# The last row tile of a matmul with layer norm: sums finished in PSUM by TensorE, two quarters scaled by ScalarE

## The chip, the cores and the metric

The kernel runs on one core of a Trainium2 chip. The metric is the device time of one execution in microseconds; of several executions the median is given. Before the change it is 246.81 us, the median of 3 runs from 246.68 to 247.35. A profile is one further execution, recorded by the hardware profiler.

## The reference

```python
m, k, n = 2048, 2048, 2048
x = np.matmul(a, b)                                # float32
mean = np.mean(x, axis=-1, keepdims=True)
var = np.var(x, axis=-1, keepdims=True)
normalized = (x - mean) / np.sqrt(var + eps)
return (gamma * normalized + beta).astype(np.float32)
```

`gamma` and `beta` have one value for each column, mean and variance one for each row; `eps` is 1e-5.

## The kernel before

The output is made in 16 row tiles of 128 rows, each in four quarters of 512 columns. A quarter is one PSUM bank, filled by 16 fp16 products (L85). The first five row tiles are worked on together while `b` arrives and is cast to fp16; from then on all of `b` lies in SBUF as `b16`, and the row tiles 5 to 15 follow one by one. Their rows of `a` are loaded with a cast by GpSimd's queue (L340) and turned by a transposing DMA on SP's queue (L407).

For each quarter `evacuate` (L95, L96) has ScalarE copy the bank to SBUF, to the tile `x`, and VectorE take its statistics. After the fourth quarter `stats` (L102 to L106) aggregates them to mean and variance (`mv`), adds eps (`ve`) and has ScalarE take the root (`sq`). The normalisation of a row tile is queued in two pieces (`queue_norm`) and run by VectorE while TensorE fills the next tile's banks. The schedule is manual: every engine runs its instructions in the order in which the program writes them, SP's stores too. The PSUM pool has eight buffers, taken in turn.

The last row tile (i = 15) has no next tile to hide behind, and `finish_row` writes its end out by hand. Quarters 0 to 2 were evacuated as usual, and `scaled` (L357) has already multiplied them by gamma in place. Quarter 3 stays in PSUM. After its last product:

- VectorE takes its statistics from PSUM (L364), then aggregates (L102) and adds eps (L104); ScalarE takes the root (L106). TensorE runs eight products of zeros meanwhile (`filler`, L236).
- VectorE centres quarter 3 and multiplies it by gamma (L367), inverts the root (`inv`, L127: `rstd`) and makes `nm` = -mean * rstd (L372).
- TensorE turns `nm` from a column to a row by a product with `ident32` (L375), and ScalarE copies the row into row 0 of `lead` (L376); row 1 of `lead` was set to ones at the start.
- For q = 1 and 2 TensorE multiplies `lead` with the rows (gamma, beta) in `rows_gb` (L380), in fp32: `w[q]` = nm * gamma + beta, as a full bank. For q = 0 VectorE makes the same as `shift` (L385) from `gamma_b` and `beta_b`, which hold gamma and beta on all partitions.
- VectorE finishes quarter 3 (`scale`, L117) and quarters 0, 1 and 2 (L390: x * rstd + w), and SP stores each quarter when it is done (`store`, L123), in the order 3, 0, 1, 2.

After the last store has landed, the program closes with waits and semaphore work.

Of the kernel before, what the change touches and what calls it, by code (L numbers as in the profile page):

```python
# [9 lines left out]
FP32 = mybir.dt.float32  # L10
FP16 = mybir.dt.float16
AluOp = mybir.AluOpType
ActFn = mybir.ActivationFunctionType
# [3 lines left out]
def kernel(  # L17
# [9 lines left out]
    nc = tc.nc  # L27
    P = 128
# [5 lines left out]
    NB = 512  # L34
# [20 lines left out]
    stat = ctx.enter_context(tc.tile_pool(name="stat", bufs=8))  # L55
    psum = ctx.enter_context(tc.tile_pool(name="psum", bufs=8, space=bass.MemoryType.PSUM))
# [4 lines left out]
    zeros = konst.tile([P, NB], FP16)  # L61
    eps_t = konst.tile([P, 1], FP32)
# [6 lines left out]
    xs = [None] * n_mt  # L69
    bnst = [None] * n_mt  # L70
    acc = {}

    def bank(name):
        return psum.tile([P, NB], FP32, tag="ps", name=name)
# [25 lines left out]
    def stats(i):  # L100
        mv = stat.tile([P, 2], FP32, tag="mv", name=f"mv{i}")
        nc.vector.bn_aggr(mv, bnst[i])  # L102
        ve = stat.tile([P, 1], FP32, tag="ve", name=f"ve{i}")
        nc.vector.tensor_tensor(ve, mv[:, 1:2], eps_t, AluOp.add)  # L104
        sq = stat.tile([P, 1], FP32, tag="sq", name=f"sq{i}")
        nc.scalar.activation(sq, ve, ActFn.Sqrt)  # L106
        return mv, sq
# [7 lines left out]
    def scale(i, q, rstd):  # L115
        qs = ds(q * NB, NB)
        nc.vector.scalar_tensor_tensor(  # L117
            xs[i][:, qs], xs[i][:, qs], rstd, beta_b[:, qs],
            AluOp.mult, AluOp.add)

    def store(i, q0, nq):
        s = ds(q0 * NB, nq * NB)
        nc.sync.dma_start(out[ts(i, P), s], xs[i][:, s])  # L123

    def inv(i, sq):
        rstd = stat.tile([P, 1], FP32, tag="rstd", name=f"rstd{i}")
        nc.vector.reciprocal(rstd, sq)  # L127
        return rstd
# [105 lines left out]
    def filler(n, to=None):  # L234
        for _ in range(n):
            nc.tensor.matmul(warm if to is None else to, zeros[:, 0:P], zeros, start=True, stop=True)  # L236
# [106 lines left out]
    rows_gb = [stg.tile([2, 2, NB], FP32, tag="st", name=f"gb{h}") for h in (0, 1)]  # L343
    ident32 = stg.tile([P, P], FP32, tag="st", name="ident32")
    nc.vector.tensor_copy(ident32, ident)
    shift = stg.tile([P, NB], FP32, tag="st", name="shift")
    lead = konst.tile([2, P], FP32)
    nc.vector.memset(lead, 1.0)
    for h in (0, 1):
        for m, vec in enumerate((gamma, beta)):  # L350
            nc.sync.dma_start(
                rows_gb[h][m:m + 1, :, :],
                vec[ds(h * NH, NH)].rearrange("(o t n) -> o t n", o=1, t=2))

    def scaled(i, q):
        qs = ds(q * NB, NB)
        nc.vector.tensor_tensor(xs[i][:, qs], xs[i][:, qs], gamma_b[:, qs], AluOp.mult)  # L357

    def finish_row(i):


        q3 = ds(3 * NB, NB)
        last_acc = acc[i, 3]
        nc.vector.bn_stats(bnst[i][:, 3, :], last_acc)  # L364
        filler(8, bank("warm2"))
        mv, sq = stats(i)
        nc.vector.scalar_tensor_tensor(  # L367
            xs[i][:, q3], last_acc, mv[:, 0:1], gamma_b[:, q3],
            AluOp.subtract, AluOp.mult)
        rstd = inv(i, sq)  # L370
        nm = stat.tile([P, 1], FP32, tag="nm", name="nm")
        nc.vector.scalar_tensor_tensor(  # L372
            nm, mv[:, 0:1], -1.0, rstd, AluOp.mult, AluOp.mult)
        nm_ps = psum.tile([1, P], FP32, tag="ps", name="nm_ps")
        nc.tensor.matmul(nm_ps, nm, ident32, start=True, stop=True)  # L375
        nc.scalar.copy(lead[0:1, :], nm_ps)  # L376
        w = {}
        for q in (1, 2):
            w[q] = bank(f"w{q}")
            nc.tensor.matmul(  # L380
                w[q], lead, rows_gb[q // 2][:, q % 2, :], start=True, stop=True)
        scale(i, 3, rstd)
        store(i, 3, 1)
        q0 = ds(0, NB)
        nc.vector.scalar_tensor_tensor(  # L385
            shift, gamma_b[:, q0], nm, beta_b[:, q0], AluOp.mult, AluOp.add)
        w[0] = shift
        for q in range(3):
            qs = ds(q * NB, NB)
            nc.vector.scalar_tensor_tensor(  # L390
                xs[i][:, qs], xs[i][:, qs], rstd, w[q], AluOp.mult, AluOp.add)
            store(i, q, 1)

    def quarter(i, q):
        for kt in range(n_kt):
# [20 lines left out]
    for i in range(R, n_mt):  # L416
        last = i == n_mt - 1
        turn_ahead(i + 2)
        for q in range(n_nb):
            quarter(i, q)  # L420
            if last and q == n_nb - 1:
                break
            evacuate(i, q)
            if q < n_nb - 1:
                drain(1)
            if last:
                scaled(i, q)
        if last:
            drain(len(backlog))
            finish_row(i)  # L430
        else:
            close(i)
# [35 lines left out]
```

## Time and profile before

| | us |
|---|---|
| median of 3 runs (lowest, highest) | 246.81 (246.68, 247.35) |
| the profiled execution | 246.63 |
| its span, from the first to the last instruction | 244.6 |
| TensorE busy | 236.8 (97%) |
| VectorE busy | 175.2 (72%) |
| ScalarE busy | 52.6 (21%) |
| GpSimd busy | 7.2 (3%) |
| start of the last tile's last statistics (L364) | 235.06 |
| issue of the last store | 240.83 |

All times in the profile are counted from the start of the span. The 246.63 us hold the span and some 2 us around it. Engines are named PE (TensorE; PEld its weight loads), DVE (VectorE), ACT (ScalarE), POOL (GpSimd) and SP, whose queue issues the stores. A row of the timeline gives start, duration, engine, line and operation, what it writes and reads, and in brackets the idle time before it with what ended it. The chain of waits goes back from the last instruction: at each step to what released it, or to the instruction before it on its engine. The granted clock of TensorE is a share of its full speed, 0.992 over the whole span.

### The profile page before, as it was taken

The page shows a single profiled execution, that of the slowest core. Times are in us where ns is not written, and L with a number is a line of the kernel's source. Part 1 is how long each engine was busy: PE and PEld are TensorE (multiplying, and loading weights), DVE is VectorE, ACT ScalarE, POOL GpSimd, SP SyncE. Part 2 cuts the span into 40 slices and gives each one's busy share as a digit, 9 for nine tenths or more (in the row PEclk, how much of TensorE's full clock was granted, in tenths as well). Part 3 has the DMA queues.
Part 4 walks back from the last instruction along what each step waited for, and adds up shares of the span by engine and source line. Part 5 has one row for each costly group of instructions (what it writes and reads, how often), then busy time and mean ns, then how long its engine had stood idle before and what let it go on. Part 6 is the DMA issues. An engine that isn't in the chain of part 4 may idle for free.

```text
span 244.6 us, 2975 instructions
## 1 busy us (share of the span) xinstructions
PE 236.8 (97%) x1137; PEld 108.0 (44%) x1137; DVE 175.2 (72%) x310; ACT 52.6 (21%) x96; POOL 7.2 (3%) x17
## 2 busy tenths in 40 slices
PE   7899999999999999999999999999999999999982
PEld 2344555444444444444444444444444444444430
DVE  1554554949997679999999995937557391947873
ACT  2457446400000011112111211112111211112100
POOL 0000000000300100000000000000000000000000
PEclk9999999999999999999999999999999999999996
DMA  4999999999999999899979897683907144120405
GB/s 125 398 386 385 388 387 385 316 357 375 331 271 179 158 131 201 196 316 205 263 189 283 147 298 222 149 200 71 256 4 190 68 123 137 74 97 0 175 1 172
DMA packets 41190, 52.64 MB, mean 215 GB/s; under 512 B 24404, under 2 KB 24404, under 8 KB 40920
## 3 DMA queue, kind: packets, MB, share of 16 engines
q1 hardware_dynamic: 39592, 46.68, 60.5%
q0 software_dynamic: 1584, 5.77, 15.4%
q8 instruction: 9, 0.15, 0.2%
q14 instruction: 5, 0.04, 0.0%
HBM read 35.67 MB, written 16.78 MB: 214 GB/s over the span
## 4 chain that ended last, share of the span: by engine, by line
PE 94%; DMA 2%; DVE 1%; ACT 0%; SPq 0%; issue 0%
PE acc L85 90%; DMA st<-in_a_dram 2%; PE tps L243 2%; PE w L380 1%; PE warm L236 1%; DVE x L390 0%; DVE bnst L364 0%; DVE x L367 0%; ACT at L245 0%; DVE a16s L186 0%; SPq L198 0%; PE nm_ps L375 0%; SPq L184 0%; DVE mv L102 0%; ACT lead L376 0%
## 5 line engine op out<-in xcount | busy, mean ns | idle before, releaser
L85 PE MATMUL acc<-b,at 128*128 128x512 f16 x1024 | 223.5, 379 | 0.7 <-DVE b L199 0.4
L85 PEld LDWEIGHTS <-at 128*128 128x128 f16 x1024 | 99.7, 98 | 119.7 <-ACT at L245 2.1
L96 DVE BATCH_NORM_STATS2 bnst<-x 128x6 f32<-128x512 f32 x48 | 33.0, 690 | 34.1 <-ACT x L95 33.9
L95 ACT COPY x<-acc 128x512 f32<-128x512 f32 x48 | 28.1, 586 | 107.8 <-PE acc L85 107.8
L117 DVE SCALAR_TENSOR_TENSOR x<-x,rstd,beta_b 128x512 f32<-128x512 f32 x61 | 43.1, 748 | 0.5
L111 DVE SCALAR_TENSOR_TENSOR x<-x,mv,gamma_b 128x512 f32<-128x512 f32 x60 | 42.1, 743 | 0.0
L205 DVE CAST b<-stb 128x1024 f16<-128x1024 f32 x30 | 20.4, 687 | 13.0 <-DMA stb<-in_b_dram 12.9
L106 ACT ACTIVATE sq<-ve 128x1 f32<-128x1 f32 x16 | 3.2, 203 | 55.5 <-DVE ve L104 55.5
L245 ACT COPY at<-tps 128x512 f16<-128x512 f16 (+1 forms) x14 | 10.8, 768 | 14.1 <-PE tps L243 14.0
L265 DVE TENSOR_TENSOR x<-acc,x 128x512 f32<-128x512 f32 x15 | 10.3, 686 | 3.0 <-PE acc L85 2.7
L266 DVE BATCH_NORM_STATS2 bnst<-x 128x6 f32<-128x512 f32 x15 | 10.4, 694 | 0.5
L236 PE MATMUL warm<-zeros 128*128 128x512 f16 x27 | 9.0, 463 | 1.2 <-DVE zeros L152 1.2
L340 POOL DMA_DIRECT2D a<-in_a_dram x11 | 6.4, 587 | 91.6 <-DMA at<-a 91.3
L261 ACT COPY x<-acc 128x512 f32<-128x512 f32 x15 | 7.6, 606 | 6.0 <-PE acc L85 6.0
L243 PEld LDWEIGHTS <-a16s 128*128 128x128 f16 x80 | 5.4, 98 | 4.7 <-DVE a16s L186 2.4
L243 PE MATMUL tps<-ident,a16s 128*128 128x128 f16 x80 | 6.8, 219 | 0.4 <-DVE a16s L186 0.3
L194 DVE CAST a16s<-sta 128x1024 f16<-128x1024 f32 x6 | 4.2, 694 | 4.0 <-DMA sta<-in_a_dram 4.0
L186 DVE CAST a16s<-st 128x512 f16<-128x512 f32 x8 | 3.4, 427 | 5.0 <-DMA st<-in_a_dram 4.8
L236 PEld LDWEIGHTS <-zeros 128*128 128x128 f16 x27 | 2.9, 113 | 4.6 <-issue 2.2
L102 DVE BATCH_NORM_AGGREGATE mv<-bnst 128x2 f32<-128x24 f32 x16 | 4.2, 264 | 0.5
L199 DVE CAST b<-st 128x512 f16<-128x512 f32 x4 | 1.7, 427 | 1.8 <-DMA st<-in_b_dram 1.8
L104 DVE TENSOR_TENSOR ve<-mv,eps_t 128x1 f32<-128x1 f32 x16 | 2.6, 160 | 0.5
(26 smaller groups left out, 16.9 us busy)
## 6 DMA issues: line engine op xcount, KB each, us to landing
stb<-in_b_dram SPq DMA_DIRECT2D x30, 512.0 KB, 6.5
out_dram<-x SPq DMA_DIRECT2D x30, 512.0 KB, 3.1
a<-in_a_dram POOLq DMA_DIRECT2D x11, 512.0 KB, 6.9
sta<-in_a_dram SPq DMA_DIRECT2D x6, 512.0 KB, 6.6
st<-in_a_dram SPq DMA_DIRECT2D x8, 256.0 KB, 6.3
st<-in_b_dram SPq DMA_DIRECT2D x4, 256.0 KB, 6.1
gamma_b<-in_gamma_dram SPq DMA_DIRECT2D x1, 1024.0 KB, 8.0
beta_b<-in_beta_dram SPq DMA_DIRECT2D x1, 1024.0 KB, 10.3
```

The source lines that it names most:

```text
L85: nc.tensor.matmul(acc[i, q], at(i)[:, kt, :], b16[:, kt, ds(q * NB, NB)], start=first, stop=last,)
L95: nc.scalar.copy(xs[i][:, qs], acc[i, q])
L96: nc.vector.bn_stats(bnst[i][:, q, :], xs[i][:, qs])
L111: nc.vector.scalar_tensor_tensor(xs[i][:, qs], xs[i][:, qs], mv[:, 0:1], gamma_b[:, qs], AluOp.subtract, AluOp.mult)
L117: nc.vector.scalar_tensor_tensor(xs[i][:, qs], xs[i][:, qs], rstd, beta_b[:, qs], AluOp.mult, AluOp.add)
L205: nc.vector.tensor_copy(b16[:, k:k + 2, ds(q * NB, NB)], st)
L236: nc.tensor.matmul(warm if to is None else to, zeros[:, 0:P], zeros, start=True, stop=True)
L243: nc.tensor.transpose(t_ps[:, m, j, :], a16_of[i, c][:, ts(j, P)], ident)
L245: nc.scalar.copy(pair[i0 // 2][:, ds(i0 % 2, n), ds(c * KC, KC), :], t_ps)
L261: nc.scalar.copy(xs[p][:, ds(q * NB, NB)], acc.pop((p, q)))
L265: nc.vector.tensor_tensor(xs[p][:, qs], acc[p, q], xs[p][:, qs], AluOp.add)
L266: nc.vector.bn_stats(bnst[p][:, q, :], xs[p][:, qs])
```

## The change

It concerns `finish_row` and what prepares it. With s = sqrt(var + eps), the result is (x * gamma - mean * gamma + s * beta) / s. For quarters 1 and 2 the bracket is now formed in PSUM: a product of zeros opens the bank `y_ps[q]` (L373), ScalarE copies the already multiplied quarter over it (L374, L382), and TensorE adds the product of `lead` with `rows_gb` (L384). `lead` now holds the rows mean and s, which come from one transposition of the tile `mv` (L380, L381), and the gamma rows of `rows_gb` get their sign changed by GpSimd at the start (L353). The root is written in place of the variance, with eps as its bias (L378). ScalarE then multiplies the banks by `rstd` on the way to SBUF (L398, L404). Quarters 3 and 0 stay with VectorE, and `nm` is made after quarter 3 is done. The stores go out in the order 3, 1, 0, 2. There are two products of zeros to open the banks and four fillers in place of eight fillers. Lines here are those of the changed file.

```diff
     lead = konst.tile([2, P], FP32)
-    nc.vector.memset(lead, 1.0)
     for h in (0, 1):
         for m, vec in enumerate((gamma, beta)):
             nc.sync.dma_start(
                 rows_gb[h][m:m + 1, :, :],
                 vec[ds(h * NH, NH)].rearrange("(o t n) -> o t n", o=1, t=2))
+        nc.gpsimd.tensor_scalar(
+            rows_gb[h][0:1, :, :], rows_gb[h][0:1, :, :], -1.0, None, AluOp.mult)
+
+    y_ps = {}
...
         nc.vector.bn_stats(bnst[i][:, 3, :], last_acc)
-        filler(8, bank("warm2"))
-        mv, sq = stats(i)
+        for q in (1, 2):
+            y_ps[q] = bank(f"y{q}")
+            nc.tensor.matmul(y_ps[q], zeros[:, 0:P], zeros, start=True, stop=False)
+        nc.scalar.copy(y_ps[1], xs[i][:, ds(NB, NB)])
+        filler(4, bank("warm2"))
+        mv = stat.tile([P, 2], FP32, tag="mv", name="mv_last")
+        nc.vector.bn_aggr(mv, bnst[i])
+        nc.scalar.activation(mv[:, 1:2], mv[:, 1:2], ActFn.Sqrt, bias=eps_t)
+        ms_ps = psum.tile([2, P], FP32, tag="ps", name="ms_ps")
+        nc.tensor.matmul(ms_ps, mv, ident32, start=True, stop=True)
+        nc.scalar.copy(lead, ms_ps)
+        nc.scalar.copy(y_ps[2], xs[i][:, ds(2 * NB, NB)])
+        for q in (1, 2):
+            nc.tensor.matmul(
+                y_ps[q], lead, rows_gb[q // 2][:, q % 2, :], start=False, stop=True)
         nc.vector.scalar_tensor_tensor(
             xs[i][:, q3], last_acc, mv[:, 0:1], gamma_b[:, q3],
             AluOp.subtract, AluOp.mult)
-        rstd = inv(i, sq)
-        nm = stat.tile([P, 1], FP32, tag="nm", name="nm")
-        nc.vector.scalar_tensor_tensor(
-            nm, mv[:, 0:1], -1.0, rstd, AluOp.mult, AluOp.mult)
-        nm_ps = psum.tile([1, P], FP32, tag="ps", name="nm_ps")
-        nc.tensor.matmul(nm_ps, nm, ident32, start=True, stop=True)
-        nc.scalar.copy(lead[0:1, :], nm_ps)
-        w = {}
-        for q in (1, 2):
-            w[q] = bank(f"w{q}")
-            nc.tensor.matmul(
-                w[q], lead, rows_gb[q // 2][:, q % 2, :], start=True, stop=True)
+        rstd = inv(i, mv[:, 1:2])
         scale(i, 3, rstd)
         store(i, 3, 1)
+        nm = stat.tile([P, 1], FP32, tag="nm", name="nm")
+        nc.vector.scalar_tensor_tensor(
+            nm, mv[:, 0:1], -1.0, rstd, AluOp.mult, AluOp.mult)
         q0 = ds(0, NB)
         nc.vector.scalar_tensor_tensor(
             shift, gamma_b[:, q0], nm, beta_b[:, q0], AluOp.mult, AluOp.add)
-        w[0] = shift
-        for q in range(3):
-            qs = ds(q * NB, NB)
-            nc.vector.scalar_tensor_tensor(
-                xs[i][:, qs], xs[i][:, qs], rstd, w[q], AluOp.mult, AluOp.add)
-            store(i, q, 1)
+        nc.scalar.activation(
+            xs[i][:, ds(NB, NB)], y_ps[1], ActFn.Copy, scale=rstd)
+        store(i, 1, 1)
+        nc.vector.scalar_tensor_tensor(
+            xs[i][:, q0], xs[i][:, q0], rstd, shift, AluOp.mult, AluOp.add)
+        store(i, 0, 1)
+        nc.scalar.activation(
+            xs[i][:, ds(2 * NB, NB)], y_ps[2], ActFn.Copy, scale=rstd)
+        store(i, 2, 1)
```

More of the change, by code (lines that the diff above doesn't have):

```diff
@@ L369, in finish_row @@
             AluOp.subtract, AluOp.mult)
-        rstd = inv(i, sq)
+        rstd = inv(i, mv[:, 1:2])
+        scale(i, 3, rstd)
+        store(i, 3, 1)
         nm = stat.tile([P, 1], FP32, tag="nm", name="nm")
@@ L373, in finish_row @@
             nm, mv[:, 0:1], -1.0, rstd, AluOp.mult, AluOp.mult)
-        nm_ps = psum.tile([1, P], FP32, tag="ps", name="nm_ps")
-        nc.tensor.matmul(nm_ps, nm, ident32, start=True, stop=True)
-        nc.scalar.copy(lead[0:1, :], nm_ps)
-        w = {}
-        for q in (1, 2):
-            w[q] = bank(f"w{q}")
-            nc.tensor.matmul(
-                w[q], lead, rows_gb[q // 2][:, q % 2, :], start=True, stop=True)
-        scale(i, 3, rstd)
-        store(i, 3, 1)
         q0 = ds(0, NB)
```

## The prediction

> **What bounds the kernel now.** I read the busy line and the forty slices first. TensorE is busy for 97% of the span and every slice but the first and the last few is full, so up to about 235 us only TensorE's work counts. The chain that ended last says the same: 90% of the span is products of L85. The change touches nothing of that; it rewrites what follows the last product. So the question is one of some nine microseconds at the end, and the view to read is the chain of waits in order of time, from its last piece of L85 on (start, duration, what):
>
> ```profile
> 214.94 20.09 PE acc L85 x93
> ...
> 235.06 0.71 DVE bnst L364
> ...
> 235.79 0.27 DVE mv L102
> ...
> 236.08 0.16 DVE ve L104
> 236.24 0.66 DVE x L367
> ...
> 237.31 0.39 PE nm_ps L375 x2
> ...
> 237.73 0.26 ACT lead L376
> ...
> 238.04 1.99 PE w L380 x4
> ...
> 240.06 0.75 DVE x L390
> ```
>
> The reader is to see one serial path: statistics of the last quarter, the row's mean and 1/sqrt, a transposition on TensorE (nm_ps), a copy (lead), 1.99 us of fp32 products (w), one VectorE pass, one store. The timeline fills in what runs beside it:
>
> ```profile
> 236.34 0.20 ACT L106 ACTIVATE sq<-ve 128x1 f32<-128x1 f32 x1 [4.15 <-DVE ve L104]
> 236.82 0.15 DVE L127 RECIPROCAL rstd<-sq 128x1 f32<-128x1 f32 x1
> 237.01 0.16 DVE L372 SCALAR_TENSOR_TENSOR nm<-mv,rstd 128x1 f32<-128x1 f32 x1
> 237.09 0.75 DVE L117 SCALAR_TENSOR_TENSOR x<-x,rstd,beta_b 128x512 f32<-128x512 f32 x1
> ...
> 237.75 0.75 DVE L385 SCALAR_TENSOR_TENSOR shift<-gamma_b,nm,beta_b 128x512 f32<-128x512 f32 x1
> ```
>
> and SP's own rows give the last store:
>
> ```profile
> 240.83 0.33 SPq L123 DMA_DIRECT2D out_dram<-x  x1
> ```
>
> The four last stores are issued at 237.86, 239.31, 239.97 and 240.83. The first three land 2.45, 2.63 and 2.69 us later; the last, at their 2.62, at 243.45. The span ends at 244.6, so about 1.15 us of closing work follows the last landing whatever the kernel does before it. The transfers' own row, in forty slices of the stretch 237.5 to 244.6, is the other thing to see:
>
> ```profile
> GB/s 0 0 0 0 0 0 92 358 404 369 254 0 0 0 69 346 381 381 358 381 323 300 323 231 346 312 335 219 127 0 0 0 0 0 0 0 0 0 0 0
> ```
>
> The quarter stored first moves alone at up to 404 GB/s; the other three follow each other from 240.0 to 242.65 with no gap. That stream is already nearly closed, which limits what an earlier issue can win.
>
> **The change, step by step.**
>
> *Statistics to transposition.* The add of eps (L104) goes; ScalarE takes it as the bias of the root. The mean and root are then transposed as they stand, so neither 1/sqrt nor nm is on the way to TensorE. Aggregation ends at 236.05. The root began 0.10 after its producer (236.24 to 236.34) and took 0.20: now 236.15 to 236.35. The transposition began 0.14 after nm and took 0.38; the first weights have two columns instead of one, which I cost at nothing: 236.49 to 236.87. ScalarE's copy to lead took 0.26 after 0.04, two partitions instead of one: 236.91 to 237.17. Before it ended at 237.99, so the products start 0.82 earlier.
>
> *Ahead of that.* TensorE now runs two zeroing products and four fillers instead of eight fillers, 0.216 us apart (the eight start 234.85 to 236.37), so it is free by 236.35, before 236.49. A copy of quarter 1 into PSUM stands in ScalarE's queue ahead of the root. It can start when the first zeroing product is done, near 235.30. No row has ScalarE writing a whole quarter to PSUM. Nearest are ScalarE's copies out of PSUM of the same size, 0.586 us; bounds are 0.20 (the root's fixed part) and 1.01 (the 128x1024 copy). I take 0.59: it ends at 235.9, 0.25 before the root needs the engine. At 1.01 the root is late by some 0.2. The copy of quarter 2 follows lead: 237.17 to 237.76; only the second product waits for it, at about 238.3. Both are covered.
>
> *Products.* The same two fp32 products with two rows: four passes, 1.98 in all, the first two done after 1.12. That they add to PSUM instead of starting there I cost at nothing, as L85 adds in fifteen of sixteen products. Started at 237.22, y1 is done at 238.34, y2 at 239.20 (w was done at 240.02).
>
> *The scaling.* ScalarE now does quarters 1 and 2, VectorE 3 and 0. A scaled ScalarE pass of this shape has no row. The copy at 0.586 and the one-element root at 0.203 bound it: 0.59 below, and the root plus a whole copy, 0.79, above. I take 0.63, nearer to the copy. Quarter 1: 238.38 to 239.01. Quarter 2: 239.24 to 239.87, against 240.06 to 240.81.
> [...]
> [...]
>
> *VectorE.* Without L104 and nm ahead, the centring of quarter 3 starts at 236.08, 1/sqrt at 236.75, its scaling runs 236.93 to 237.68 (before 237.84), store at 237.70. Then nm, shift and quarter 0: 237.60, 237.79 and 238.58 to 239.33. Quarter 0 is 0.05 later than before, but no longer ahead of two more passes.
>
> *SP's queue.* The order is now quarters 3, 1, 0, 2, each issue 0.33 us; the closest two issues in the trace, at 63.13 and 63.48, lie 0.35 apart, and I allow 0.42. Quarter 1 goes at 239.03; quarter 0 waits behind it and goes at 239.45; quarter 2 at 239.89. The last issue is **0.94 us earlier** than 240.83.
>
> *Early parts.* VectorE loses one memset. GpSimd gets two sign changes of 1x1024 behind its last load issue, which is over by 163.4. No row shows their length; even 10 us each would be done 50 us before TensorE reads them. Should they slow VectorE there, its idle time takes it up: from the slice of 163 us on its digits in the page's forty slices are 3, 7, 5, 5.
>
> *Landing.* Quarters 1, 0 and 2 are now issued within 0.86 us, not 1.52. 262,144 bytes at some 385 GB/s (the lone store's full slices are 358 to 404) take 0.68 us, so they queue. The first would land at 239.03 + 2.55 = 241.58, the last not before 241.58 + 2 x 0.68 = 242.94. With the 0.73 and 0.79 that lay between landings in the trace it is 243.10. Against 243.45 that is 0.51 or 0.35 us. If the transfers overlap as if each were alone, it is 239.89 + 2.62 = 242.51, a gain of the whole 0.94. I take **0.55**, near the queued price.
>
> **The sum.** Profiled execution: 246.63 us, span 244.6. 246.63 - 0.55 = 246.08. The median shown is 246.81, 0.18 above that execution, so on the median's scale the forecast is **246.25 us**, 0.23% faster. About 0.3%, or 0.74 us, is what a measurement of this kernel can tell from no change.
>
> **The rivals.**
>
> 1. *The transfers don't queue.* For: the stores are 2.45 to 2.69 us each, of which only 0.7 is data. Against: the slices from 240.0 to 242.65 show no gap at a spacing of 0.66 and 0.86. Gain 0.94: 245.87.
> 2. *ScalarE eats the gain.* It is now serial from the root to quarter 2: five passes. At 0.79 for each scaling, and 1.01 for each copy into PSUM, the root is 0.2 late and the last scaling 0.16 longer; of the 0.94 remain 0.58 at the issue, and a stream that is then less dense lands 0.2 to 0.4 earlier, or none if landings stretch. 246.4 to 246.8.
> 3. *TensorE's clock falls before the products are done: slower.* The granted clock is 1.00 in 237 to 240 and 0.57 on average in 240 to 244.6, which is one full speed to 240.6 and half after it, only 0.6 after the last fp32 pass; those passes did not hold it. Two fillers fewer may let it fall earlier. Each pass then takes 0.43 more; the gain at the issue is gone from the third slow pass on (a fall before about 237.8), and with all four slow y2 ends 1.7 later, the store leaves 0.8 after 240.83: 247.6. Against: in the trace the fall came 3.9 us after the last filler; the same delay from 236.3 is 240.2, a whole 1.0 after y2 is done. [...]
> 4. *It does not do what it says*: an early part shifts, or the path ends elsewhere (quarter 0's store, say) and nothing is won: 246.8.
>
> **Chances.** Forecast with queued stores, 245.95 to 246.55: 0.52. Rival 1: 0.24. Rival 2: 0.14. Rival 3: 0.05. Rival 4: 0.05. Faster by over 0.3% (below 246.07) is nearly all of rival 1 and a part of the forecast: 0.30. Slower by over 0.3% is rival 3 and some of 4: 0.08. Within: 0.62. For 8 in 10 the range leaves out rival 3 and the ends: from 245.65 (245.87 less the 0.18 between median and execution, rounded down) to 246.95 (nothing won, and a run a little above the median).
>
> **What would show it.** [...] Then the slices of the transfers: a closed stream of three stores near 385 GB/s, the last landing near 242.9. It is wrong if the passes are 0.86 apart (rival 3), if the scaled passes are near 0.8 or the root starts after 236.3 (rival 2), or if the last landing keeps 2.6 us from its issue (rival 1).

## The result, and the profile after

The changed kernel takes 246.66 us (median of 21 runs, 246.35 to 246.97), the kernel before 246.93 us on the same chips (21 runs, 246.65 to 247.8). The ratio is 0.9985 with a 95% interval from 0.9979 to 0.9991: a gain of 0.37 us, between 0.22 and 0.52 (the two medians alone differ by 0.27). That is inside the 0.3% within which the prediction called the two equal; the interval shows that it is a gain all the same.

The span of the profiled execution, 244.7 us, is no shorter than before. The reason lies at the other end: its last tile's statistics start at 235.37 instead of 235.06, because the first loads came 0.3 us later (the first block of `b` landed at 6.76 instead of 6.45). In the twelve profiles of this case that start lies between 235.06 and 235.84, in kernels with almost the same code up to there. What follows it repeats far better: in two profiles of the changed kernel the last landing comes 8.141 and 8.142 us after it. So everything below is counted **from the start of the last statistics (T)**. From T to the end of the span it was 9.57 us; now it is 9.31.

The chain of waits of the changed kernel, in order of time (start, duration, what), from the last products of L85 on:

```profile
214.83 20.52 PE acc L85 x95
...
235.37 0.71 DVE bnst L370
...
236.10 0.27 DVE mv_last L377
...
236.40 0.30 ACT mv_last L378
...
236.75 0.39 PE ms_ps L380 x2
...
237.16 0.26 ACT lead L381
237.43 0.14 issue
237.56 1.96 PE y L384 x4
...
239.55 0.69 ACT x L404
```

Between the root (mv_last L378) and the transposition nothing of VectorE is left, and the last piece is ScalarE's scaled pass. The products start 2.19 us after T instead of 2.98 and end 4.14 after it instead of 4.96. SP's rows give the last issue:

```profile
240.31 0.40 SPq L123 DMA_DIRECT2D out_dram<-x  x1
```

That is T + 4.94, against T + 5.78 before: 0.84 us won at the issue. Now the transfers, in forty slices of 0.175 us from 237.6 to 244.6:

```profile
GB/s 0 0 0 0 0 0 0 257 386 386 386 82 0 0 0 328 374 398 398 328 410 328 351 363 258 257 293 222 176 12 0 0 0 0 0 0 0 0 0 0
```

Fifteen slices in a row are filled, from 240.2 to 242.8, at up to 410 GB/s first and under 300 at the end. The landing of a store is its event in the trace; for the last store it shows only as the end of SP's last wait for a store: 243.51, T + 8.14, against T + 8.40. Of 0.84 us at the issue, 0.26 arrive at the landing. The last store now takes 3.2 us from issue to landing, not 2.6.

### The profile page after: what moved, and what is told of

It is laid out like the page before. It is cut to its first block, busy times and chain, and to the rows that moved or that the text cites. A ratio compares the mean times of both kernels' runs of the same rounds, so it can differ in the third digit from the quotient of the medians.

```text
span 244.7 us, 2976 instructions
## 1 busy us (share of the span) xinstructions
PE 236.4 (97%) x1135; PEld 107.8 (44%) x1135; DVE 173.7 (71%) x306; ACT 55.1 (23%) x100; POOL 12.6 (5%) x19
## 4 chain that ended last, share of the span: by engine, by line
PE 94%; DMA 2%; ACT 1%; DVE 1%; SPq 0%; issue 0%
PE acc L85 90%; DMA st<-in_a_dram 2%; PE tps L243 2%; PE y L384 1%; PE warm L236 1%; DVE bnst L370 0%; ACT x L404 0%; ACT at L245 0%; DVE a16s L186 0%; SPq L198 0%; PE ms_ps L380 0%; SPq L184 0%; ACT mv_last L378 0%; DVE mv_last L377 0%; ACT lead L381 0%
## 5 line engine op out<-in xcount | busy, mean ns | idle before, releaser
L85 PE MATMUL acc<-b,at 128*128 128x512 f16 x1024 | 223.5, 379 | 1.1 <-DVE b L199 0.8
L85 PEld LDWEIGHTS <-at 128*128 128x128 f16 x1024 | 99.7, 98 | 119.7 <-ACT at L245 2.1
L236 PE MATMUL warm<-zeros 128*128 128x512 f16 x23 | 8.2, 478 | 1.2 <-DVE zeros L152 1.2
L353 POOL TENSOR_SCALAR gb<-gb 1x1024 f32<-1x1024 f32 x2 | 5.5, 2764 | 0.0
```

Of the source, the lines that this page charges most:

```text
L85: nc.tensor.matmul(acc[i, q], at(i)[:, kt, :], b16[:, kt, ds(q * NB, NB)], start=first, stop=last,)
```

## The experiments

**Theory S**: the last three stores form a closed stream, that is, their transfers follow each other without an empty slice. Its start and what each store adds set the last landing; when the last of them is issued hardly matters. **Rival L**: a landing comes a set time after its own issue, and this time grew from 2.6 to 3.2 for another reason. The table has what the profiles show, in us after T: the issues of the last tile's stores in their order with the quarter, the last landing, and the timed result; each ratio is to runs of the kernel before that were taken with the row's own runs.

| kernel | issues (quarter) | last landing | median, ratio to before (95%) |
|---|---|---|---|
| before | 2.80 (3), 4.25 (0), 4.92 (1), 5.78 (2) | 8.40 | 246.93 |
| changed | 2.66 (3), 4.03 (1), 4.46 (0), 4.94 (2) | 8.14 | 246.66, 0.9985 (0.9979 to 0.9991) |
| e1 | 2.66 (3), 4.04 (1), 4.89 (2) | 7.38 | 245.59, 0.9948 (0.9935 to 0.9961) |
| e2 | 2.67 (3), 4.31 (0), 4.97 (1), 5.63 (2) | 8.45 | 246.89, 0.9994 (0.9985 to 1.0002) |
| e3 | 2.67 (3), 4.04 (1), 4.46 (0), 4.94 (2) | 8.16 | 246.76, 0.9990 (0.9980 to 1.0001) |
| e4 | 2.67 (3), 3.24 (1), 4.31 (0), 4.74 (2) | 7.52 | 245.94, 0.9953 (0.9942 to 0.9965) |
| e5 | 2.67 (3), 4.04 (1), 4.46 (0), 5.47 (2) | 8.16 | 246.64, 0.9987 (0.9978 to 0.9995) |
| e6 | 2.66 (3), 3.24 (1), 3.82 (2), 4.31 (0) | 7.47 | 245.83, 0.9958 (0.9946 to 0.9971) |
| e7 | 2.67 (3), 4.04 (1), 4.31 (0), 5.18 (2) | 8.21 | 246.42, 0.9980 (0.9970 to 0.9989) |
| e8 | 2.67 (3), 4.31 (0), 4.74 (1), 5.21 (2) | 8.46 | 246.78, 0.9989 (0.9974 to 1.0004) |
| e9, changed again | 2.67 (3), 4.04 (1), 4.46 (0), 4.94 (2) | 8.14 | 246.67, 0.9985 (0.9975 to 0.9996) |
| e10, e7 again | 2.67 (3), 4.04 (1), 4.31 (0), 5.18 (2) | 8.21 | 246.53, 0.9974 (0.9962 to 0.9986) |

### e5: the last store issued later

```diff
+    spare = stg.tile([P, NB], FP32, tag='st', name='spare')
...
         store(i, 0, 1)
+        nc.scalar.activation(spare, y_ps[2], ActFn.Copy, scale=rstd)
         nc.scalar.activation(
             xs[i][:, ds(2 * NB, NB)], y_ps[2], ActFn.Copy, scale=rstd)
```

> The changed kernel with one useless scaled pass of 0.69 us on ScalarE ahead of the scaling of quarter 2 (into a spare tile), so that only the last store is issued later, by 0.6 to 0.7 us. Theory S: the last store then finds the transfers free and lands about 2.6 us after its issue, so that the end moves by 0 to 0.15 us: 246.65 to 246.8. Rival L: the landing moves with the issue, 247.25 to 247.35.

The timeline of ScalarE shows the useless pass, and SP's rows the late issue:

```profile
239.49 0.69 ACT L405 ACTIVATE spare<-y,rstd 128x512 f32<-128x512 f32 x1 [0.17 <-PE y L385]
240.08 0.68 ACT L406 ACTIVATE x<-y,rstd 128x512 f32<-128x512 f32 x1
```

```profile
240.78 0.33 SPq L123 DMA_DIRECT2D out_dram<-x  x1
```

Its transfers, in forty slices from 237.6 to 244.6, are a closed stream, as in the changed kernel:

```profile
GB/s 0 0 0 0 0 0 59 339 386 398 293 24 0 0 82 363 374 374 386 386 351 293 293 363 281 328 293 211 117 0 0 0 0 0 0 0 0 0 0 0
```

T is 235.31 here: the issue is at T + 5.47, 0.54 later than in the changed kernel, and the last landing at 8.16, 0.02 later. The time did not move (246.64 against 246.66). Rival L is out: over half a microsecond of the gain at the issue was worth nothing.

### e1: one store fewer in the stream

```diff
             xs[i][:, q0], xs[i][:, q0], rstd, shift, AluOp.mult, AluOp.add)
-        store(i, 0, 1)
```

> The changed kernel without the store of quarter 0 of the last row tile (a quarter of that tile is not written); all arithmetic is as it was. Theory S (the last landing is set by the stream of three stores that queue behind each other): quarter 2, issued at about the same moment, now follows one store instead of two and lands about 2.6 us after its issue instead of 3.2: the end comes 0.5 to 0.7 us earlier, about 246.05. Rival L (a late store's landing takes 3.2 us for its own reasons, such as the issue or the receipt): nothing moves, 246.6 to 246.7.

Its transfers, in forty slices from 237.4 to 244.4, and the last store's issue line (KB, us to landing):

```profile
GB/s 0 0 0 0 0 0 82 363 386 386 281 0 0 0 117 374 410 410 187 129 386 374 386 223 0 0 0 0 0 0 0 0 0 0 0 0 0 0 0 0
```

```profile
out_dram<-x SPq DMA_DIRECT2D x1, 256.0 KB, 2.5
```

Three humps at 370 to 410 GB/s, each a store, with a dip between the second and third, where the changed kernel has one plateau that sinks. The last store lands 2.47 us after its issue, like the lone first one (2.44), and 0.76 us earlier than in the changed kernel. The timed gain was larger than expected (a median of 245.59, where 246.05 was); the tail in the profile explains 0.7 of the 1.07 us between the medians of this kernel and the changed one, and the rest I can't place.

### e8: the same work, the stream started later

```diff
-        store(i, 1, 1)
         nc.vector.scalar_tensor_tensor(
             xs[i][:, q0], xs[i][:, q0], rstd, shift, AluOp.mult, AluOp.add)
         store(i, 0, 1)
+        store(i, 1, 1)
```

> The changed kernel with the stores queued in the order 3, 0, 1, 2; nothing else differs. Quarter 1, ready 4.0 us after the start of the last statistics, now waits on SP behind quarter 0, ready at 4.3: issues at 4.3, 4.75 and 5.15 instead of 4.0, 4.45 and 4.95. Theory S (the stream of the last three stores is closed, so its start decides): the last landing comes 0.25 to 0.3 us later, and the gain of the change is gone: 246.85 to 246.95. Rival L (the last issue decides, 2.6 us before its landing): 5.15 + 2.6 is still before the 8.14 of the changed kernel, so the time stays at 246.65 or falls.

The first of the three is issued 0.28 us later than in the changed kernel, and the last landing is 0.32 later, at 8.46, 0.06 past where it was before the change. The median lies 0.12 above the changed kernel's, below what I expected, and the intervals overlap, so the verdict rests on the profile. The last landing is not at 5.21 + 2.6 = 7.8, as L has it.

### e2: who scales

```diff
-        nc.scalar.activation(
-            xs[i][:, ds(NB, NB)], y_ps[1], ActFn.Copy, scale=rstd)
-        store(i, 1, 1)
         nc.vector.scalar_tensor_tensor(
             xs[i][:, q0], xs[i][:, q0], rstd, shift, AluOp.mult, AluOp.add)
         store(i, 0, 1)
-        nc.scalar.activation(
-            xs[i][:, ds(2 * NB, NB)], y_ps[2], ActFn.Copy, scale=rstd)
+        nc.vector.tensor_scalar(
+            xs[i][:, ds(NB, NB)], y_ps[1], rstd, None, AluOp.mult)
+        store(i, 1, 1)
+        nc.vector.tensor_scalar(
+            xs[i][:, ds(2 * NB, NB)], y_ps[2], rstd, None, AluOp.mult)
         store(i, 2, 1)
```

> The changed kernel with the scaling of quarters 1 and 2 given back to VectorE, in the order 3, 0, 1, 2; sums in PSUM, transposition and products as changed. If the gain at the issue comes from ScalarE sharing the passes, VectorE is the bound again: its passes end 4.3, 5.0 and 5.7 us after the start of the last statistics, the last store goes out within 0.1 us of where it did before the change (5.78), and the time is that of before, 246.8 to 246.95. Rival P (the gain comes from the earlier transposition and the sums in PSUM, whoever scales): 246.6 to 246.7, like the change.

The chain of waits, from the centring of quarter 3 to the last pass (in the row DVEq L477 the chain names VectorE's sequencer; what ran there is the scaling of quarter 1, L401, from 239.27 to 240.02):

```profile
236.11 0.75 DVE x L386
...
236.96 0.75 DVE x L117
...
237.82 0.76 DVE shift L396
...
238.60 0.75 DVE x L398
239.36 0.66 DVEq L477
240.02 0.66 DVE x L404
```

With the early transposition and the sums in PSUM but six big passes in a row on VectorE, this stretch of the chain is VectorE's alone; TensorE's products are no longer on it. The last store goes out at 5.63, 0.15 us sooner than before the change (0.1 was expected), and yet it lands at 8.45, 0.05 later, as the first of the three is issued 0.06 later. The time is as before. The earlier transposition by itself buys nothing: ScalarE's share of the passes turns it into an earlier stream.

### e7 and e10: two queues

```diff
-        store(i, 1, 1)
+        nc.scalar.dma_start(out[ts(i, P), ds(1 * NB, NB)], xs[i][:, ds(1 * NB, NB)])
...
-        store(i, 2, 1)
+        nc.scalar.dma_start(out[ts(i, P), ds(2 * NB, NB)], xs[i][:, ds(2 * NB, NB)])
```

> The changed kernel with the stores of quarters 1 and 2 issued from ScalarE's own DMA queue instead of SP's; quarters 3 and 0 stay with SP. Quarter 1 goes at about 4.05, quarter 0 at 4.3, quarter 2 at about 5.1, since ScalarE issues quarter 1 before it scales quarter 2. Theory S with the 16 transfer engines or the memory as the bound: two queues share them, the last landing stays within 0.15 us, 246.55 to 246.8. Rival Q (one queue's own order and overhead is the bound): stores of two queues overlap, the last lands 0.3 to 0.5 us earlier, 246.15 to 246.35.

> The changed kernel as it is, on the same chip as the next one, so that the two can be set side by side: 246.6 to 246.75, and a last landing 8.1 to 8.2 us after the start of the last statistics.

> The same kernel as e7: the stores of quarters 1 and 2 from ScalarE's own queue. Theory S, with transfer engines or memory as the bound: within 0.1 us of the changed kernel on the same chip, last landing 8.1 to 8.3. Rival Q (SP's queue is the bound, and the profile of e7 was one of its late executions): 0.2 to 0.3 us below the changed kernel, last landing 7.7 to 8.0.

The changed kernel repeats as expected (e9: 246.67 and 8.14). In both profiles of the two queues the last landing is at 8.21, 0.07 after that of one queue. Quarter 0's store, issued by SP at 4.31 with only quarter 3's ahead of it on its own queue, still takes 3.2 us to land; before the change, in the same place on the queue, it took 2.6. So in these profiles SP's order is not what holds the stores up; where they meet was not shown. Whether the two queues change the time is unclear: the medians are 0.24 and 0.14 us below the changed kernel's, between what theory S and rival Q expected, the intervals overlap, and the profiles show no gain.

### e3: the clock

```diff
-        filler(4, bank("warm2"))
```

> The changed kernel without its four fillers; the two products of zeros that open the banks stay. TensorE's last full products end 0.4 us after the start of the last statistics. If the clock falls no sooner than 3.4 us after them (3.8, and the fp32 passes are done at 4.14), at most one pass is slower: 246.65 to 246.75. Rival C (the fillers keep the clock up): it falls before or in the fp32 passes, which are then 0.86 us apart instead of 0.43; the last issue is up to 1.7 us late and the time 247 to 248.

Two stretches of its profile (their length; busy time and instructions of PE, PEld, DVE, ACT and POOL; granted clock; share and GB/s of the transfers):

```profile
237.00:240.00 3.00, 2.03 (x5) 0.66 (x4) 2.50 (x6) 1.92 (x4) 0.00 (x0) 1.00 0.23 87
240.00:244.60 4.60, 0.00 (x0) 0.00 (x0) 0.00 (x0) 0.19 (x1) 0.00 (x0) 0.59 0.52 171
```

The clock stays at 1.00 while the fp32 passes run, and they take 1.95 us in all, as in the changed kernel. The 0.59 of the second stretch puts the fall at an estimated 240.8, full speed until then and after it the 0.50 that the profiles of before and after show from 240.7 on. In the profile the fillers are not needed. The 3.4 us of the expectation were my assumption: before the change the clock fell 3.88 us after the last full product, and 3.98 in the changed kernel. The runs spread from 246.5 to 247.51, wider than the 21 of the changed kernel, but its runs in e9 spread nearly as far (246.42 to 247.35); whether the clock fell early in some of them was not seen.

### e4 and e6: an earlier stream

The other lever by theory S is the stream's start, and that waits for the first product. In e4 `lead` and the rows (-gamma, beta) are fp16, so a product is one pass; VectorE makes the fp16 rows with their sign in row tile 13, in place of GpSimd's sign changes. e6 has in addition the order 3, 1, 2, 0.

```diff
-    lead = konst.tile([2, P], FP32)
+    lead = konst.tile([2, P], FP16)
+    sign = konst.tile([2, 1], FP32)
+    nc.vector.memset(sign, 1.0)
+    nc.vector.memset(sign[0:1, :], -1.0)
+    gb16 = stg.tile([2, 4, NB], FP16, tag="st", name="gbh")
...
-                y_ps[q], lead, rows_gb[q // 2][:, q % 2, :], start=False, stop=True)
+                y_ps[q], lead, gb16[:, q, :], start=False, stop=True)
...
+        if i == n_mt - 3:
+            for h in (0, 1):
+                nc.vector.tensor_scalar(
+                    gb16[:, 2 * h:2 * h + 2, :], rows_gb[h], sign, None, AluOp.mult)
```

> The changed kernel with lead and the rows (-gamma, beta) as fp16, so that each product takes one pass of 0.22 us instead of two of 0.43 (mean and root, gamma and beta are rounded to fp16 in these products); the change of sign is done by VectorE in row tile 13, and the stores go out in the order 3, 1, 0, 2 as in the change. Quarter 1 is issued about 3.3 us after the start of the last statistics instead of 4.0, so the stream of stores starts earlier; quarter 0 goes at 4.3, quarter 2 behind it at 4.75. Theory S: the last landing comes 0.5 to 0.8 us earlier, 245.9 to 246.15, since the stores are spread wider. Rival L (3.2 us after the last issue): the last issue moves by 0.2 alone, 246.45.

> The kernel with one-pass fp16 products (e4), with the stores and scalings in the order 3, 1, 2, 0: issues at 2.67, 3.24, 3.85 and 4.31 instead of 2.67, 3.24, 4.31 and 4.74 (mean and root, gamma and beta are rounded to fp16 in these products, as in e4). Theory S: the stream is closed from the first store on, each store adds 0.7 to 0.8 us to the landing before it, so the last lands at 7.2 to 7.5, 0 to 0.3 us before that of e4: 245.65 to 245.95. Rival L: 2.6 us after the last issue, 6.95: 245.35.

The timeline of e4, whose T is 235.22, from lead on:

```profile
237.01 0.26 ACT L383 CAST lead<-ms_ps 2x128 f16<-2x128 f32 x1 [0.47 <-PE ms_ps L382]
...
237.32 0.85 PE L386 MATMUL y<-gbh,lead 2*128 2x512 f16 x2 [0.35 <-ACT lead L383]
237.75 0.69 ACT L400 ACTIVATE x<-y,rstd 128x512 f32<-128x512 f32 x1
```

ScalarE scales quarter 1 from T + 2.53 instead of 3.32. In e4 the last store is issued only 0.20 us earlier than in the changed kernel, yet it lands 0.62 earlier, because the stream starts 0.8 earlier. e6 issues its last store another 0.42 earlier and lands 0.06 earlier. Its transfers in slices from 237.4 show why:

```profile
GB/s 0 0 0 0 0 0 82 363 374 363 386 375 374 281 386 375 222 269 339 410 398 281 234 269 176 35 0 0 0 0 0 0 0 0 0 0 0 0 0 0
```

There is no empty slice left from the first store to the last: the megabyte of the last tile is one stream. Both kernels beat the changed one and the one before: 245.94 and 245.83 us.

## Why the prediction was right, step by step

- *Statistics to transposition*: right. The root was forecast 1.09 after T and came at 1.03; lead was done at 2.05 (forecast 2.11); the products started at 2.19 (2.16) and ended at 4.14 (4.14). That the end fits so well is partly luck, as small errors cancel: the root took 0.29 us, not 0.20, but the transposition began 0.05 after it, not 0.14; and 0.14 instead of 0.05 passed between lead and the first product, which the earlier root and products of 1.95 instead of 1.98 made up for. In that gap the trace has a wait record of TensorE, 0.05 us at 237.45, that the product before the change did not have (it now waits for GpSimd as well, whose work was done at 169.2). That this wait is the cause was not tried by itself, but in e4, without it, the gap is 0.06.
- *ScalarE's copies into PSUM*, unseen before: 0.59 and 0.57 us, as taken. Both stayed covered.
- *The scaling*: 0.69, where 0.63 was taken. The rows of ScalarE (behind the bar: busy us, mean ns, idle before):

```profile
L398 ACT ACTIVATE x<-y,rstd 128x512 f32<-128x512 f32 x1 | 0.7, 688 | 0.8 <-PE y L384 0.8
L374 ACT COPY y<-x 128x512 f32<-128x512 f32 x1 | 0.6, 592 | 3.1 <-PE y L373 3.1
L378 ACT ACTIVATE mv_last<-mv_last,eps_t 128x1 f32<-128x1 f32 x1 | 0.3, 294 | 0.2 <-DVE mv_last L377 0.2
```

  The root with eps as its bias takes 91 ns more than the 203 of the old root; the pass scaled by a column takes 96 ns more than this copy into PSUM, and 102 more than the copy out of PSUM (586). My 0.63 allowed 44 ns over the copy, an estimate; in these rows a column as operand goes with 91 to 102 ns more. VectorE's scaling of the same bank takes 743 to 746 ns (e2), so ScalarE is the faster one here, by less than the copy's 586 made it look.
- *SP's queue*: issues forecast at T + 3.97, 4.39 and 4.83, measured 4.03, 4.46 and 4.94. The last is 0.84 earlier than before, not 0.94: 0.06 for the scaling, and the rest on SP, whose issues now take up to 0.40 us. The closest two issues of the trace are not the pair at 63.13, as the text has it, but one at 65.29 and 65.56, 0.27 apart; the 0.42 allowed was near the measured 0.42 and 0.48 all the same.
- *Landing*: **the step that was mis-sized.** That the stores would queue was right (e5, e1, e8), and the first of the three landed as forecast (6.52, measured 6.54). But each further store was charged 0.68 us, the lone store's data at its own rate of some 385 GB/s; they added 0.91 and 0.68, together 1.59 instead of 1.36. The 0.73 and 0.79 of the trace of before, which the text had as the price of the smaller gain, would have given 0.35; the profile shows 0.26, the timed runs 0.37 (0.22 to 0.52).
- *The sum*: 246.25 (its terms give 246.26) against 246.66. A part of that 0.41 is the base: the median of before is 246.93 over 21 runs, 0.12 above that of the three shown; the rest is the landing. 246.66 lies within the range for 8 in 10, but that range reached up to 246.95 and would have held a change worth nothing too. It lies above the 245.95 to 246.55 given to the forecast with queued stores, and in the 246.4 to 246.8 of rival 2, whose cause did not occur.
- *Rival 1*, transfers that don't queue: out, as the last store took 3.2 us from its issue and not 2.6, and by e5 because of the queue. *Rival 2*: of the 0.36 that it charged at the issue, the scalings cost 0.06; the copies into PSUM held up nothing. The root began at 236.40, after the 236.3 named as a sign of this rival, only because T itself came 0.31 later. *Rival 3*, the clock: it fell at 240.62 before the change and at 240.60 in the changed kernel, 3.88 and 3.98 us after the last full product (128x512, fp16), 0.61 and 1.09 after the last fp32 pass. In the twelve profiles it fell 3.41 to 5.12 us after the last full product, and in each of them after the last fp32 pass. What sets this delay was not shown. *Rival 4*: GpSimd's two sign changes took 2.76 us each, from 163.7 on, and ended 68 us before TensorE read the rows.

## What to carry to other kernels

At the end of a kernel, draw the transfers as a stream before pricing an earlier issue: here the last stores already followed each other without an empty slice, the start of the stream and its bytes set the end, and of the 0.84 us won at the last issue 0.26 were left at the landing. Price a store that queues by the landings' spacing in the trace (here 0.68 to 0.91 us), not by a lone store's rate (here 0.68). And compare such a tail from the last event that both kernels share: the span hid a change of 0.26 us behind 0.3 us of different starts.

## What was not expected of the hardware

- The packets of stores that followed closely were slower here: those of 2 KB took 86 to 88 ns on the mean in a store that ran alone or led the stream, and in the changed kernel 95 and 110 in the second and third; before the change 99 and 104.5, single ones up to 213. With the same bytes on two queues it is the same (87, 99, 110 in e7). A store has 128 of them, eight for each of the 16 engines if they share them evenly, so the slower ones add an estimated 0.27 us, about the 0.23 that the landing's price lacked. Why they slowed down stays open.
- The clock fell as soon with fp32 products on two rows as without them: in e4, e7 and e9 3.4 to 3.5 us after the last full product, though e7 and e9 ran 1.95 us of fp32 passes in between.
- In the two profiles of the changed kernel the last landing and the end of the span repeat within 0.02 us from T on, while T itself moves by 0.8 us over the twelve profiles.
